# Loads of a softmax in two transfers of 32 KB per partition, on fixed buffers in program order

## The chip, the cores and the metric

The kernel runs on one core of one Trainium2 chip. The metric is the device time of one execution in microseconds (us); smaller is better. An execution under the profiler shows a span about 1.8 us shorter than its device time.

## The reference

Softmax over the last axis of 16 x 256 rows of 32768 float32 values, with a temperature of 1.0:

```python
def reference(logits, temperature):        # logits: 16 x 256 x 32768 float32
    scaled = logits / temperature
    scaled = scaled - scaled.max(axis=-1, keepdims=True)
    exp_scaled = np.exp(scaled)
    return (exp_scaled / exp_scaled.sum(axis=-1, keepdims=True)).astype(np.float32)
```

It reads 537 MB and writes 537 MB, and there is no way round either.

## The kernel before

Each row is cut into two halves, which lie in neighbouring partitions. A tile is 128 partitions x 16384 values, 64 KB in a partition; there are 64 tiles and three buffers for them. A tile is loaded in one transfer, worked on in four pieces of 4096 (maximum on DVE, exponential and sum on ACT), then the factors of its rows are combined, the tile is scaled by DVE and ACT together, and stored in one transfer. Only the first tile's load and the last tile's load and store are cut into four.

```python
def load(i):                       # one transfer, except in the first and last tile
    ...
    for s, n in spans(CW, _LAST_DMA if g in (0, G - 1) else CW):
        tc.keep_in_program_order(nc.sync.dma_start(out=xs[:, s : s + n], in_=x[...]))

def exps(i):
    ...
    for j, (s, n) in enumerate(ps):                    # 4 pieces of 4096
        nc.vector.tensor_reduce(out=nm[:, k : k + 1], in_=xs[:, s : s + n], axis=X, op=A.max, negate=True)
        nc.scalar.activation(out=xs[:, s : s + n], in_=xs[:, s : s + n], func=Exp,
                             bias=nm[:, k : k + 1], scale=inv_t, accum_out=ssum[:, k : k + 1])

def scales(i):
    ...                                                # of each piece 2560 on DVE, 1536 on ACT

# order on the queue: load 0, 1, 2, store 0, then store t, load t + 2 for t = 1, 2, ...
```

All transfers are issued by SP on one queue. Each of the 16 DMA engines does its share of every transfer, in this order.

## Time and profile before

| | before |
|---|---|
| median of the first three runs | 2501.49 us (2500.46 to 2506.35) |
| busy: DVE, ACT | 63%, 55% |
| data rate over the span | 429 GB/s |
| store to store, one tile | 39.1 us |

Two views that the prediction does not show. First, from the page, the costliest group and the issues of the inner tiles; the last number of an issue line is the median time from issue to landing:

```profile
L107 DVE TENSOR_REDUCE nm<-xs 128x1 f32<-128x4096 f32 x256 | 1113.7, 4412 | 661.6 <-DMA xs<-in_logits_dram 661.6
...
out_dram<-xs SPq DMA_DIRECT2D x63, 29.8
xs<-in_logits_dram SPq DMA_DIRECT2D x62, 49.1
```

The maxima are the largest piece of compute, and DVE spends as much as 661.6 us waiting for loads. A store takes some 19 us of transfer but lands 29.8 us after its issue, so about 10 us of other work lay in the queue ahead of it. Call that its **lead**.

### The profile page before, as it was taken

Reading aid. Unit: us, or ns where it says so; the run is one execution under the profiler, and the core shown is the slowest. Engines: PE = TensorE matmul, PEld = TensorE weight load, DVE = VectorE, ACT = ScalarE, POOL = GpSimd, SP = SyncE. Lnnn points to the kernel's source line nnn. Section 1 sums busy time; section 2 is a strip of 40 time slices with the busy share of each in tenths; the row PEclk is TensorE's granted clock in tenths of the full one; section 3 lists DMA queues with packets and bytes.
Section 4 is the critical chain, followed back from the end, with each engine's and each line's share of the span. In section 5 each row is a group of like instructions: output and inputs, shape, how many; then the busy total and the mean of one; then the engine's idle time right before and its main releaser. Section 6 shows DMA issues by size and latency. Waiting matters only on the chain.

```text
span 2504.7 us, 2498 instructions
## 1 busy us (share of the span) xinstructions
DVE 1579.7 (63%) x1216; ACT 1368.7 (55%) x833; POOL 0.2 (0%) x4
## 2 busy tenths in 40 slices
DVE  6575665765656656666565665666657666576665
ACT  5464554645546455464554645546555464564655
POOL 0000000000000000000000000000000000000000
DMA  9999999999999999999999999999999999999998
GB/s 419 434 426 433 429 436 434 436 434 433 435 434 434 429 428 433 433 434 422 433 422 431 434 423 432 433 422 434 429 425 434 423 433 432 423 433 432 423 422 375
DMA packets 19748, 1073.91 MB, mean 429 GB/s; under 512 B 2192, under 2 KB 2192, under 8 KB 2192
## 3 DMA queue, kind: packets, MB, share of 16 engines
q1 hardware_dynamic: 19728, 1073.75, 99.8%
q14 instruction: 20, 0.16, 0.0%
HBM read 536.87 MB, written 536.87 MB: 429 GB/s over the span
## 4 chain that ended last, share of the span: by engine, by line
DMA 74%; DVE 14%; ACT 10%; SPq 1%; issue 0%; ACTq 0%; another core or an unknown queue 0%
DMA xs<-in_logits_dram 72%; DVE nm L107 13%; ACT xs L163 7%; ACT xs L114 3%; DMA out_dram<-xs 2%; SPq L75 1%; DVE xs L160 0%; DVE f L150 0%; ACT ee L131 0%; DVE rS L149 0%; DVE Sh L87 0%; DVE Sh L84 0%; DVE ttj L138 0%; ACTq L224 0%
## 5 line engine op out<-in xcount | busy, mean ns | idle before, releaser
L107 DVE TENSOR_REDUCE nm<-xs 128x1 f32<-128x4096 f32 x256 | 1113.7, 4412 | 661.6 <-DMA xs<-in_logits_dram 661.6
L114 ACT ACTIVATE xs<-xs,nm 128x4096 f32<-128x4096 f32 x256 | 949.1, 3708 | 1032.9 <-DVE nm L107 1032.9
L163 ACT ACTIVATE xs<-xs,f 128x1536 f32<-128x1536 f32 x256 | 382.3, 1564 | 73.5 <-DVE f L150 73.5
L160 DVE TENSOR_SCALAR xs<-xs,f 128x2560 f32<-128x2560 f32 x256 | 380.2, 1549 | 2.6 <-DVE f L150 0.4
L138 DVE CUSTOM_DVE_ANT_0 ttj<-ee,ssum 128x4 f32<-128x4 f32 x64 | 10.4, 162 | 222.4 <-ACT ee L131 222.4
L114 ACT ACTIVATION_READ_ACCUMULATOR xs<-xs,nm 128x1 f32 x256 | 47.8, 187 | 0.0
L131 ACT ACTIVATE ee<-nm,nMh 128x4 f32<-128x4 f32 x64 | 18.0, 282 | 0.0
L150 DVE TENSOR_SCALAR f<-ee,rS 128x4 f32<-128x4 f32 x64 | 14.7, 229 | 2.2
L149 DVE RECIPROCAL rS<-Sh 128x1 f32<-128x1 f32 x64 | 10.5, 164 | 2.2
L87 DVE TENSOR_TENSOR Sh<-Sh 128x1 f32<-128x1 f32 x64 | 10.2, 160 | 2.2
L87 DVE TENSOR_TENSOR nMh<-nMh 128x1 f32<-128x1 f32 x64 | 10.2, 160 | 2.2
L129 DVE TENSOR_REDUCE nMh<-nm 128x1 f32<-128x4 f32 x64 | 10.1, 157 | 2.2
L84 DVE STREAM_SHUFFLE nMh<-nMh 128x1 f32<-128x1 f32 x64 | 9.7, 151 | 0.0
L84 DVE STREAM_SHUFFLE Sh<-Sh 128x1 f32<-128x1 f32 x64 | 9.7, 151 | 0.0
L114 ACT ACT_TABLE_LOAD x1 | 1.3, 1283 | 7.9 <-DMA xs<-in_logits_dram 7.9
L138 DVE DVE_READ_ACCUMULATOR2_ANT Sh<- 128x1 f32 x64 | 5.2, 82 | 0.0
L84 DVE LOAD_MASK_SELECT nMh<-nMh x64 | 0.9, 14 | 2.8
L84 DVE LOAD_MASK_SELECT Sh<-Sh x64 | 0.9, 14 | 2.7
L210 POOL MEMSET const-bfloat16-1.0<- 128x1 bf16 x1 | 0.1, 101 | 0.0
L210 POOL MEMSET const-uint8-127<- 128x1 uint8 x1 | 0.1, 101 | 0.0
L210 POOL MEMSET const-float32-0.0<- 128x1 f32 x1 | 0.1, 98 | 0.2 <-issue 0.2
L210 POOL MEMSET const-float32-1.0<- 128x1 f32 x1 | 0.1, 98 | 0.0
## 6 DMA issues: line engine op xcount, KB each, us to landing
xs<-in_logits_dram SPq DMA_DIRECT2D x8, 2048.0 KB, 27.3
out_dram<-xs SPq DMA_DIRECT2D x4, 2048.0 KB, 15.5
out_dram<-xs SPq DMA_DIRECT2D x63, 29.8
xs<-in_logits_dram SPq DMA_DIRECT2D x62, 49.1
```

The source lines that it names most:

```text
L75: nc.sync.dma_start(out=o[g * P : (g + 1) * P, c * CW + s : c * CW + s + n], in_=xs[:, s : s + n],)
L84: nc.vector.stream_shuffle(out=v[:, j + 1 : j + 2], in_=v[:, j : j + 1], mask=mask)
L87: nc.vector.tensor_tensor(out=v[:, j + 1 : j + 2], in0=v[:, j : j + 1], in1=v[:, j + 1 : j + 2], op=op,)
L107: nc.vector.tensor_reduce(out=nm[:, k : k + 1], in_=xs[:, s : s + n], axis=X, op=A.max, negate=True)
L114: nc.scalar.activation(out=xs[:, s : s + n], in_=xs[:, s : s + n], func=Exp, bias=nm[:, k : k + 1], scale=inv_t, accum_out=ssum[:, k : k + 1],
L129: nc.vector.tensor_reduce(out=nMh[:, 0:1], in_=nm, axis=X, op=A.min)
L131: nc.scalar.activation(out=ee, in_=nm, func=Exp, bias=nMh[:, n_rounds : n_rounds + 1], scale=-1.0,)
L138: nc.vector.tensor_tensor_reduce(out=ttj, in0=ee, in1=ssum, scale=1.0, scalar=0.0, op0=A.mult, op1=A.add, accum_out=Sh[:, 0:1],)
L149: nc.vector.reciprocal(out=rS, in_=Sh[:, n_rounds : n_rounds + 1])
L150: nc.vector.tensor_scalar_mul(out=f, in0=ee, scalar1=rS)
L160: nc.vector.tensor_scalar_mul(out=xs[:, s : s + cut], in0=xs[:, s : s + cut], scalar1=f[:, k : k + 1])
L163: nc.scalar.activation(out=xs[:, s + cut : s + n], in_=xs[:, s + cut : s + n], func=Copy, scale=f[:, k : k + 1],)
```

## The change

The intent: a tile's first half is worked on while its second half is still being loaded, and the schedule is written out in program order on fixed buffers instead of being left to the tile scheduler. The diff, cut to its core:

```diff
-_CW = 16384
 _BUFS = 3
-_PIECE = 4096
-_LAST_DMA = 4096
-_DVE_SHARE = 0.625
+_LOAD = 8192
+_STORE = 16384
+_PIECES = (4096, 4096, 4096, 2048, 2048)
+_ON_DVE = (4096, 4096, 2048, 0, 0)
...
+    buf = [pool.tile([P, W], fp32, tag=f"x{b}", name=f"x{b}") for b in range(_BUFS)]
...
+    def load(t: int) -> None:
+        n = _END if t in (0, G - 1) else _LOAD
+        for s in range(0, W, n):
+            nc.sync.dma_start(out=buf[t % _BUFS][:, s : s + n], in_=x[t * P : (t + 1) * P, s : s + n])
...
+    with tc.manual_schedule():
+        for t in range(_BUFS):
+            load(t)
+        for t in range(G):
+            normalise(t)
+            store(t)
+            if t and t + _BUFS - 1 < G:
+                load(t + _BUFS - 1)
```

The arithmetic is unchanged. The first two pieces lie in the first half of a tile, the other three in the second.

More of the change, by code (lines that the diff above doesn't have):

```diff
@@ L9 @@
 _SPLIT = 2
-_CW = 16384
 _BUFS = 3
-_PIECE = 4096
-_LAST_DMA = 4096
-_DVE_SHARE = 0.625
+_LOAD = 8192
+_STORE = 16384
+_PIECES = (4096, 4096, 4096, 2048, 2048)
+_ON_DVE = (4096, 4096, 2048, 0, 0)
+_END = 4096
+_END_ON_DVE = 2560
+_SETS = 3
 @with_exitstack
@@ L37 @@
     W = V // _SPLIT
-    CW = min(_CW, W)
-    C = W // CW
-    assert W * _SPLIT == V and CW * C == W and (N * _SPLIT) % P == 0
+    assert sum(_PIECES) == W and len(_PIECES) == len(_ON_DVE)
     x = xf.rearrange("n (h v) -> (n h) v", h=_SPLIT)
@@ L43, with store @@
     G = N * _SPLIT // P
-    n_chunks = G * C
+    assert G * P == N * _SPLIT
     n_rounds = _SPLIT.bit_length() - 1
-    xpool = ctx.enter_context(tc.tile_pool(name="x", bufs=_BUFS))
-    spool = ctx.enter_context(tc.tile_pool(name="stats", bufs=3))
-    slots = {}
-    stats = {}
-    def spans(total: int, step: int) -> list[tuple[int, int]]:
-        return [(s, min(step, total - s)) for s in range(0, total, step)]
-    def piece(g: int) -> int:
-        return _PIECE if g < G - 1 else min(_PIECE, _LAST_DMA)
-    def load(i: int) -> None:
-        g, c = divmod(i, C)
-        xs = xpool.tile([P, CW], fp32, tag="x", name="xs")
-        slots[i] = xs
-        for s, n in spans(CW, _LAST_DMA if g in (0, G - 1) else CW):
-            tc.keep_in_program_order(
-                nc.sync.dma_start(
-                    out=xs[:, s : s + n],
-                    in_=x[g * P : (g + 1) * P, c * CW + s : c * CW + s + n],
-                )
-            )
-    def store(i: int) -> None:
-        g, c = divmod(i, C)
-        xs = slots.pop(i)
-        for s, n in spans(CW, _LAST_DMA if g == G - 1 else CW):
-            tc.keep_in_program_order(
-                nc.sync.dma_start(
-                    out=o[g * P : (g + 1) * P, c * CW + s : c * CW + s + n],
-                    in_=xs[:, s : s + n],
-                )
+    K = max(len(_PIECES), W // _END)
+    pool = ctx.enter_context(tc.tile_pool(name="fixed", bufs=1))
+    buf = [pool.tile([P, W], fp32, tag=f"x{b}", name=f"x{b}") for b in range(_BUFS)]
+    widths = dict(nm=K, ssum=K, ee=K, f=K, ttj=K, nMh=2, Sh=2, rS=1)
+    stat = [
+        {
+            k: pool.tile([P, w], fp32, tag=f"{k}{s}", name=f"{k}{s}")
+            for k, w in widths.items()
+        }
+        for s in range(_SETS)
+    ]
+    def load(t: int) -> None:
+        n = _END if t in (0, G - 1) else _LOAD
+        for s in range(0, W, n):
+            nc.sync.dma_start(
+                out=buf[t % _BUFS][:, s : s + n],
+                in_=x[t * P : (t + 1) * P, s : s + n],
+            )
+    def store(t: int) -> None:
+        n = _END if t == G - 1 else _STORE
+        for s in range(0, W, n):
+            nc.sync.dma_start(
+                out=o[t * P : (t + 1) * P, s : s + n],
+                in_=buf[t % _BUFS][:, s : s + n],
             )
@@ L92, in combine, with normalise @@
             )
-    def exps(i: int) -> None:
-        g, c = divmod(i, C)
-        xs = slots[i]
-        ps = spans(CW, piece(g))
-        K = C * len(ps)
-        if c == 0:
-            stats[g] = tuple(
-                spool.tile([P, K], fp32, tag=f"{nm}{K}", name=nm)
-                for nm in ("nm", "ssum", "ee", "f", "ttj")
-            )
-        nm, ssum = stats[g][:2]
-        for j, (s, n) in enumerate(ps):
-            k = c * len(ps) + j
+    def normalise(t: int) -> None:
+        xs = buf[t % _BUFS]
+        if t in (0, G - 1):
+            sizes = [_END] * (W // _END)
+            on_dve = [_END_ON_DVE] * len(sizes)
+        else:
+            sizes, on_dve = _PIECES, _ON_DVE
+        K = len(sizes)
+        at = [sum(sizes[:k]) for k in range(K)]
+        st = stat[t % _SETS]
+        nm, ssum, ee, f, ttj = (st[k][:, :K] for k in ("nm", "ssum", "ee", "f", "ttj"))
+        nMh, Sh, rS = st["nMh"], st["Sh"], st["rS"]
+        for k in range(K):
+            xc = xs[:, at[k] : at[k] + sizes[k]]
             nc.vector.tensor_reduce(
-                out=nm[:, k : k + 1], in_=xs[:, s : s + n], axis=X, op=A.max, negate=True
+                out=nm[:, k : k + 1], in_=xc, axis=X, op=A.max, negate=True
             )
@@ L114, in exps @@
             nc.scalar.activation(
-                out=xs[:, s : s + n],
-                in_=xs[:, s : s + n],
+                out=xc,
+                in_=xc,
                 func=Exp,
@@ L121, in exps @@
             )
-    def factors(g: int) -> None:
-        nm, ssum, ee, f, ttj = stats[g]
-        nMh = spool.tile([P, 1 + n_rounds], fp32, tag="nMh", name="nMh")
-        Sh = spool.tile([P, 1 + n_rounds], fp32, tag="Sh", name="Sh")
-        rS = spool.tile([P, 1], fp32, tag="rS", name="rS")
-        with tc.high_priority():
-            nc.vector.tensor_reduce(out=nMh[:, 0:1], in_=nm, axis=X, op=A.min)
-            combine(nMh, A.min)
-            nc.scalar.activation(
-                out=ee,
-                in_=nm,
-                func=Exp,
-                bias=nMh[:, n_rounds : n_rounds + 1],
-                scale=-1.0,
-            )
-            nc.vector.tensor_tensor_reduce(
-                out=ttj,
-                in0=ee,
-                in1=ssum,
-                scale=1.0,
-                scalar=0.0,
-                op0=A.mult,
-                op1=A.add,
-                accum_out=Sh[:, 0:1],
-            )
-            combine(Sh, A.add)
-            nc.vector.reciprocal(out=rS, in_=Sh[:, n_rounds : n_rounds + 1])
-            nc.vector.tensor_scalar_mul(out=f, in0=ee, scalar1=rS)
@@ L152, in scales @@
-    def scales(i: int) -> None:
-        g, c = divmod(i, C)
-        xs = slots[i]
-        f = stats[g][3]
-        ps = spans(CW, piece(g))
-        for j, (s, n) in enumerate(ps):
-            k = c * len(ps) + j
-            cut = int(n * _DVE_SHARE) // 512 * 512
-            nc.vector.tensor_scalar_mul(
-                out=xs[:, s : s + cut], in0=xs[:, s : s + cut], scalar1=f[:, k : k + 1]
-            )
-            nc.scalar.activation(
-                out=xs[:, s + cut : s + n],
-                in_=xs[:, s + cut : s + n],
-                func=Copy,
-                scale=f[:, k : k + 1],
-            )
@@ L170 @@
-    order = [("L", i) for i in range(min(_BUFS, n_chunks))] + [("S", 0)]
-    for i in range(1, n_chunks):
-        order.append(("S", i))
-        if i + _BUFS - 1 < n_chunks:
-            order.append(("L", i + _BUFS - 1))
-    nxt = 0
-    done = -1
-    loaded = 0
-    for kind, i in order:
-        if kind == "L":
-            load(i)
-            loaded = i + 1
-        else:
-            g = i // C
-            if g > done:
-                while nxt < (g + 1) * C:
-                    assert nxt < loaded
-                    exps(nxt)
-                    nxt += 1
-                factors(g)
-                done = g
-            scales(i)
-            store(i)
+        nc.vector.tensor_reduce(out=nMh[:, 0:1], in_=nm, axis=X, op=A.min)
@@ new lines, in normalise @@
+        combine(nMh, A.min)
+        nc.scalar.activation(
+            out=ee, in_=nm, func=Exp, bias=nMh[:, n_rounds : n_rounds + 1], scale=-1.0
+        )
+        nc.vector.tensor_tensor_reduce(
+            out=ttj,
+            in0=ee,
+            in1=ssum,
+            scale=1.0,
+            scalar=0.0,
+            op0=A.mult,
+            op1=A.add,
+            accum_out=Sh[:, 0:1],
+        )
+        combine(Sh, A.add)
+        nc.vector.reciprocal(out=rS, in_=Sh[:, n_rounds : n_rounds + 1])
@@ new lines, in normalise @@
+        nc.vector.tensor_scalar_mul(out=f, in0=ee, scalar1=rS)
+        for k in range(K):
+            a, b, c = at[k], at[k] + on_dve[k], at[k] + sizes[k]
+            if b > a:
+                nc.vector.tensor_scalar_mul(
+                    out=xs[:, a:b], in0=xs[:, a:b], scalar1=f[:, k : k + 1]
+                )
+            if c > b:
+                nc.scalar.activation(
+                    out=xs[:, b:c], in_=xs[:, b:c], func=Copy, scale=f[:, k : k + 1]
+                )
+    with tc.manual_schedule():
[6 more added lines that the diff above has]
+                load(t + _BUFS - 1)
```

## The prediction

> **What bounds the kernel now.** I read the page from the top: busy shares, then the DMA row, then the chain that ended last, and after that the waits and one stretch of the timeline. The busy shares say that no engine is the bound (DVE 63%, ACT 55%); the DMA rows say what is.
>
> ```profile
> DVE 1579.7 (63%) x1216; ACT 1368.7 (55%) x833; POOL 0.2 (0%) x4
> ...
> DMA  9999999999999999999999999999999999999998
> ...
> q1 hardware_dynamic: 19728, 1073.75, 99.8%
> ...
> HBM read 536.87 MB, written 536.87 MB: 429 GB/s over the span
> ...
> DMA 74%; DVE 14%; ACT 10%; SPq 1%; issue 0%; ACTq 0%; another core or an unknown queue 0%
> ```
>
> One queue keeps the 16 DMA engines occupied for 99.8% of the span, with no slice below 9 tenths but the last. The chain names DVE and ACT for 24%, but a chain follows one path only; while it runs through DVE the DMA engines are busy too. Whether compute really holds up the transfers has to be seen in one steady tile. The timeline there:
>
> ```profile
> 1008.18 0.33 SPq L75 DMA_DIRECT2D out_dram<-xs  x1
> 1008.56 0.43 SPq L64 DMA_DIRECT2D xs<-in_logits_dram  x1
> 1018.79 17.40 DVE L107 TENSOR_REDUCE nm<-xs 128x1 f32<-128x4096 f32 x4 [10.72 <-DMA xs<-in_logits_dram]
> ...
> 1041.30 5.94 DVE L160 TENSOR_SCALAR xs<-xs,f 128x2560 f32<-128x2560 f32 x4
> 1041.36 5.97 ACT L163 ACTIVATE xs<-xs,f 128x1536 f32<-128x1536 f32 x4 [1.15 <-DVE f L150]
> 1047.36 0.33 SPq L75 DMA_DIRECT2D out_dram<-xs  x1
> 1047.74 0.43 SPq L64 DMA_DIRECT2D xs<-in_logits_dram  x1
> 1057.69 17.40 DVE L107 TENSOR_REDUCE nm<-xs 128x1 f32<-128x4096 f32 x4 [10.45 <-DMA xs<-in_logits_dram]
> ```
>
> Call a row block of 128 x 16384 values (8.39 MB) a tile. A tile lands at 1018.79, is computed in 28.57 us, and its store is issued at 1047.36. The load issued at 1008.56 lands only at 1057.69. So when the store is put into the queue, the queue still has 1057.69 - 1047.36 = 10.3 us of loading ahead of it: compute is early by that much. The wait views agree:
>
> ```profile
> DVE nm L107 <- DMA xs<-in_logits_dram: 661.6, 65, 22.3
> ...
> SPq L75 <- DVE xs L160: 2385.2, 67, 38.7
> ...
> SPq L64 <- DMA out_dram<-xs: 13.0, 2, 10.8
> ```
>
> DVE waits for loads 65 times, some 10 us a tile. SP waits nearly always for the scaling, which is harmless because the queue behind it is full; it waits for a buffer to be stored only twice, at the start. The kernel is bound by the rate of its transfers, from the first packet to the last.
>
> **The steady period.** Stores go out at 1008.18 and 2415.83, 36 tiles apart: 39.10 us a tile. How long does a transfer take undisturbed? At the start the waits of DVE end at 7.89, 12.78, 17.67 and 22.57, so a 2.1 MB transfer (16 KB a partition) takes 4.90 us; the next, 8.39 MB (64 KB), lands at 41.91: 19.34 us. A load and a store would then be 2 x 19.34 = 38.68. The missing 0.42 us a tile (27 us in 64 tiles) is the change of direction: in the trace's packet records a 64 KB packet takes 2.418 us nearly always, and the longer ones (up to some 3.7 us) are mostly the last of a load with a store behind it. The semaphore records show too that the 16 DMA engines drift apart: from 0.3 us between first and last at the start to about 8.5 us from the middle on. The last of them sets the time, and it never runs dry.
>
> **What the Trainium skill says.** Three places. "DMA: Bandwidth & Descriptors", Where 436 GB/s comes from: a fabric ceiling of 435.2 GB/s. This trace agrees: 8.39 MB in 19.34 us is 433.7 GB/s. At the ceiling 1073.74 MB would need 2467 us (an estimate from the page's figure), 1.4% under the time now, so a gain over 2% isn't there to be had with the same bytes. Same page, Why small descriptors are slow: a fixed overhead for each packet of about 3 cycles. The trace agrees that there is one: packets of 16 KB take 611 ns and of 64 KB 2418 ns; on a straight line that is about 9 ns fixed. "Perfetto Trace Analysis", DMA Optimizations: splitting may let work start sooner "if DMA engines are generally idle". Here they are not, so the condition fails.
>
> **The change part by part.**
> 1. *Loads in two transfers of 32 KB a partition.* 62 tiles change (the first and the last keep four of 16 KB). On the line through 4.90 us for 2.1 MB and 19.34 us for 8.39 MB, 4.19 MB takes 4.90 + (19.34 - 4.90)/3 = 9.71 us, two of them 19.42: 0.08 us more than one. The packet records give the same: 16 x (611 + (2418 - 611)/3 = 1213 ns) + 2 x 9 for the semaphores, against 8 x 2418 + 9, is +73 ns. All of it lies on the bound: 62 x 0.08 = **+5 us**.
> 2. *Compute starts on the first half.* Two reductions of 4.41 us (8.8 us) then run in the 9.7 us before the second half lands. After it lands: reductions of 4096, 2048, 2048, the last three exponentials, factors, scaling. By the rows now, an ACT pass takes 3.71 us for 4096 and (on the line with 1.56 for 1536) about 2.0 for 2048. So: first reduction done at 4.4, exponentials with their reads until 4.4 + 3.9 + 2.2 + 2.2 = 12.7, factors until about 14.1, scaling 6.0 (ACT 3 x 1.99; DVE 2 x 2.35 + 1.28): about **20 us** instead of 28.6. Stores are issued 8.5 us earlier in the period, with about 19 us in the queue ahead of them instead of 10.3. As the queue never was empty, this is worth **0 us**; DVE and ACT only idle longer.
> 3. *More instructions:* 5 pieces for 4, fewer scale operations. DVE a tile: 3 x 4.41 + 2 x 2.28 + 5.98 + about 1.5 = 25.3 us against 24.7; ACT 22.3 against 21.4. Both stay far below 39.1: **0 us**.
> 4. *Fixed buffers, program order.* Still three buffers of 64 KB, and the SP order store t, load t+2 is the old one. A load needs the store of the tile two before the last stored one landed, some 20 us after the last landing. That is now about when the next store goes out (20 us), so SP will wait for stores in nearly every tile, briefly. At that moment the queue still holds most of a load and a whole store: **0 us**.
> 5. *Start and end.* The first four loads and the last four stores keep their sizes; the last engine had no gap there before: **0 us**.
>
> Sum: 2501.5 + 5 = 2506.5; I put 2507.
>
> **The rivals.**
> *The change of direction gets cheaper or dearer.* It is 27 us now. The last packet before a store is half as long; if the extra time goes with packet size, 13 us come back and the time is about 2493. Against it: what is lost looks like a cost of turning round, and there are as many turns as before. The other way: with the store waiting in the queue for longer (19 us), or the engines drifting further apart (by my model the leaders can be 39.1 - 20 - 2 = 17 us ahead, now 39.1 - 28.6 - 2 = 8.5, which matches what is seen), the last engine could lose more. The first turn in the trace, with its store queued 23 us early, cost some 1 us. Half as much again each turn would be +13: about 2520.
> *A wait takes the place of the one removed.* SP stuck on a load's buffer holds back the store behind it. For this to cost anything the queue must run dry for the last engine, and it has over 15 us in it. If it did happen at 1 us a tile: 2570.
> *DVE or ACT becomes the bound.* At 25.3 and 22.3 us of 39.1 this can't be, unless program order makes them wait in turn; 20 us after a landing leaves 19 to spare.
> *The transfers were held up by compute after all,* so that the extra slack buys back the 27 us: about 2479. The leaders do wait for stores to be issued, but the last engine doesn't, and only it counts. I give it little.
>
> **Range and chances.** The known term is +5; the unknown one is the turn, within about -13 and +13; repeated runs before spread by 6 us. So 2495 to 2520 for 8 in 10. Faster by over 2% (below 2451) is under the ceiling's 2467: 0.5%. Slower by over 2% (above 2552) needs a stall I can't find: 2.5%. The rest is within 2%.
>
> **What would show it.** Right: DMA still 9 tenths throughout; packets 19728 + 62 x 144 = 28656 on the queue; halves landing 9.7 us apart; a period of about 39.2 us; store issued about 20 us after the second half; SP waits for stores in some 60 places, short. DVE's wait for loads split in two per tile. Wrong: a period under 38.9 (turns cheaper) or over 39.5 (turns dearer, drift), DMA slices below 9 tenths (starved), or SP waiting longer for stores than the queue is deep.

## More of the kernel before

Every run here was at a granted clock of 1.0. The experiments ran in three sets, each on its own chip (1 to 4, 5 to 8, 9 to 11), and runs of the kernel before were mixed into each: 2495.97 to 2509.48 us over all of them. Differences of a few us are safe within a set, less so between sets.

Second, the busy times in two stretches of the steady part; the columns are the stretch, its length, busy us of DVE, ACT and POOL with their counts, granted clock, DMA share and GB/s:

```profile
400.00:1500.00 1100.00, 698.39 (x534) 605.05 (x367) 0.00 (x0) 1.00 1.00 432
1500.00:2400.00 900.00, 568.29 (x438) 491.88 (x301) 0.00 (x0) 1.00 1.00 430
```

The DMA share is 1.00 in both, and still the rate differs a little. A share of 1.00 says that packets were under way, not that they moved as fast as they can.

## The result, and the profile after

The changed kernel took 2496.48 us in the median of four runs (2496.34 to 2496.77), the kernel before 2502.43 us (2500.46 to 2506.35). The ratio is 0.9974, with a 95% interval of 0.9957 to 0.9992: a quarter of a per cent faster, and much steadier. (The fastest of all runs of the kernel before, 2495.97 us, is as fast; it is its other runs that are slower. A ratio here is the mean time of one kernel's fast runs over that of the other's in the same rounds, so it is not quite the ratio of the medians quoted.) The profiled spans were 2504.7 and 2494.7 us. The profiled run of the kernel before, 2506.49 us, was slower than its four timed ones, so the 10 us between the profiles are more than the usual gain of some 6.

The queues and the chain after, from the page:

```profile
q1 hardware_dynamic: 28656, 1073.75, 99.7%
q14 instruction: 22, 0.18, 0.0%
HBM read 536.87 MB, written 536.87 MB: 430 GB/s over the span
...
DMA 73%; ACT 13%; DVE 12%; another core or an unknown queue 1%; SPq 1%; issue 0%; ACTq 0%
```

There are 28656 packets instead of 19728, just the 62 x 144 more that were expected, and DMA is as full as before. The steady tile in the timeline after:

```profile
1017.04 8.80 DVE L103 TENSOR_REDUCE nm<-x 128x1 f32<-128x4096 f32 x3 [0.93 <-DMA x<-in_logits_dram]
...
1030.55 5.81 DVE L139 TENSOR_SCALAR x<-x,f 128x4096 f32<-128x4096 f32 x3
1030.61 5.79 ACT L143 ACTIVATE x<-x,f 128x2048 f32<-128x2048 f32 x3 [1.15 <-DVE f L135]
1036.43 0.34 SPq L71 DMA_DIRECT2D out_dram<-x  x1
1036.82 0.91 SPq L63 DMA_DIRECT2D x<-in_logits_dram  x2
1046.06 8.74 DVE L103 TENSOR_REDUCE nm<-x 128x1 f32<-128x4096 f32 x2 [9.70 <-DMA x<-in_logits_dram]
...
1055.74 8.80 DVE L103 TENSOR_REDUCE nm<-x 128x1 f32<-128x4096 f32 x3 [0.94 <-DMA x<-in_logits_dram]
...
1075.13 0.34 SPq L71 DMA_DIRECT2D out_dram<-x  x1
```

The second half of a tile lands at 1017.04 and its store is issued 19.4 us later, at 1036.43. The next tile's second half lands at 1055.74, so this store has a lead of 19.3 us instead of 10.3. From store to store it is 38.70 us. Who waited, DVE first and then the queue of SP:

```profile
DVE nm L103 <- DMA x<-in_logits_dram: 673.3, 128, 17.6
```

```profile
SPq L71 <- DVE x L139: 1780.2, 67, 33.5
SPq L71 <- DMA x<-in_logits_dram: 571.0, 60, 18.0
SPq L63 <- DMA out_dram<-x: 28.0, 11, 15.3
```

DVE waits for loads as long as before in all, only twice a tile. SP waits for a store to land 11 times, 28 us in all. And the two stretches of the steady part again:

```profile
400.00:1500.00 1100.00, 700.81 (x548) 608.83 (x401) 0.00 (x0) 1.00 1.00 433
1500.00:2400.00 900.00, 570.95 (x439) 493.81 (x324) 0.00 (x0) 1.00 1.00 433
```

The second stretch moves 433 GB/s, where it was 430: there, at a DMA share that never left 1.00, is the gain.

**Where it lies.** Each transfer ends with one semaphore increment from each of the 16 DMA engines, and the trace records them. The time between the last increments of two transfers is what the last engine needed. Its undisturbed time for a tile is 38.63 us with one load and 38.70 with two (the shortest tiles of these profiles and those below). What it lost on top:

- Before: some 28 us in all. Ten steps of about 0.95 us, some 250 us apart, and the rest, about 18 us, in losses of 0.1 to 0.7 us (1.0 in the first) in most of the other loads, mostly in the packet or two ahead of the store.
- After: some 13 us. About 4 us in the first eight tiles, then hardly anything but nine steps of 1.0 us.

So 14 us of losses at the turn from load to store went and the added packets took 4 us back: 10 us, as the spans say. The timeline agrees: over the last 59 stores a tile took 39.07 us before and 38.89 after, 10.6 us in all. But why are the losses gone? The same turn from load to store still happens in every tile.

The increments show one more thing. The 16 engines start together and drift apart; the time between the first and the last is called the **distance** below. Before, the first was ahead of the last by 0.3 us at the start, and from the middle on by 8 to 9.6 us, no further. After, the distance grows by 1.0 us at each step and reaches 12.3 us. So before, something held the first ones back.

### The profile page after: what moved, and what is told of

It is laid out like the page before. It is cut to its first block, busy times and chain, and to the rows that moved or that the text cites. A ratio compares the mean times of both kernels' runs of the same rounds, so it can differ in the third digit from the quotient of the medians.

```text
span 2494.7 us, 2743 instructions
## 1 busy us (share of the span) xinstructions
DVE 1581.4 (63%) x1216; ACT 1367.8 (55%) x895; POOL 0.2 (0%) x4
## 3 DMA queue, kind: packets, MB, share of 16 engines
q1 hardware_dynamic: 28656, 1073.75, 99.7%
## 4 chain that ended last, share of the span: by engine, by line
DMA 73%; ACT 13%; DVE 12%; another core or an unknown queue 1%; SPq 1%; issue 0%; ACTq 0%
DMA x<-in_logits_dram 64%; DVE nm L103 11%; DMA out_dram<-x 8%; ACT x L110 7%; ACT x L143 6%; SPq L71 0%; DVE f L135 0%; ACT ee L120 0%; DVE rS L134 0%; DVE Sh L82 0%; DVE ttj L123 0%; DVE Sh L79 0%; SPq L63 0%; ACTq L185 0%
## 5 line engine op out<-in xcount | busy, mean ns | idle before, releaser
L103 DVE TENSOR_REDUCE nm<-x 128x1 f32<-128x4096 f32 x318 | 1123.3, 3581 | 673.3 <-DMA x<-in_logits_dram 673.3
L110 ACT ACTIVATE x<-x,nm 128x4096 f32<-128x4096 f32 x318 | 965.4, 3036 | 1020.9 <-DVE nm L103 1020.9
L143 ACT ACTIVATE x<-x,f 128x2048 f32<-128x2048 f32 (+1 forms) x194 | 370.9, 1975 | 73.7 <-DVE f L135 73.7
L139 DVE TENSOR_SCALAR x<-x,f 128x4096 f32<-128x4096 f32 (+2 forms) x194 | 372.2, 1975 | 2.3
L123 DVE CUSTOM_DVE_ANT_0 ttj<-ee,ssum 128x5 f32<-128x5 f32 (+1 forms) x64 | 10.6, 166 | 196.7 <-ACT ee L120 196.7
L110 ACT ACTIVATION_READ_ACCUMULATOR x<-x,nm 128x1 f32 x318 | 59.3, 186 | 0.0
L120 ACT ACTIVATE ee<-nm,nMh 128x5 f32<-128x5 f32 (+1 forms) x64 | 18.1, 284 | 0.0
L135 DVE TENSOR_SCALAR f<-ee,rS 128x5 f32<-128x5 f32 (+1 forms) x64 | 14.8, 231 | 2.2
L118 DVE TENSOR_REDUCE nMh<-nm 128x1 f32<-128x5 f32 (+1 forms) x64 | 10.1, 158 | 2.2
```

Source lines behind the costliest of these rows:

```text
L103: nc.vector.tensor_reduce(out=nm[:, k : k + 1], in_=xc, axis=X, op=A.max, negate=True)
L110: nc.scalar.activation(out=xc, in_=xc, func=Exp, bias=nm[:, k : k + 1], scale=inv_t, accum_out=ssum[:, k : k + 1],)
L118: nc.vector.tensor_reduce(out=nMh[:, 0:1], in_=nm, axis=X, op=A.min)
L120: nc.scalar.activation(out=ee, in_=nm, func=Exp, bias=nMh[:, n_rounds : n_rounds + 1], scale=-1.0)
L123: nc.vector.tensor_tensor_reduce(out=ttj, in0=ee, in1=ssum, scale=1.0, scalar=0.0, op0=A.mult, op1=A.add, accum_out=Sh[:, 0:1],)
L135: nc.vector.tensor_scalar_mul(out=f, in0=ee, scalar1=rS)
```

## The experiments

Theories at the start: SIZE (a turn costs in proportion to the last load packet, and that was halved), LEAD (it costs because the store is queued late) and ORDER (fixed buffers and program order did it).

**1. Undo the split of the loads alone** (load64).

```diff
-_LOAD = 8192
+_LOAD = 16384
```

> Only the split of the loads is undone (one transfer of 64 KB per partition); fixed buffers, program order and the five pieces stay. The load-to-store turn cost the last DMA engine about 16 us before and about 3 us after. Theory SIZE (the turn costs in proportion to the last load packet, 64 KB against 32 KB) and theory LEAD (it costs because the store is queued only 10 us ahead of the turn, against 19 us): both expect the turn's cost back and the 5 us of packets gone, 2501 to 2504 us, with losses of 0.1 to 0.6 us in most loads. Theory ORDER (fixed buffers and program order removed it): stays near 2491 us.

Measured: 2497.66 us, but spread over 2494.83 to 2509.60; ratio 0.9986 (0.9967 to 1.0005), so not to be told from the kernel before, whose 11 runs in this set lay between 2498.63 and 2507.51. The profile holds the hint. Between about 600 and 1500 us its tiles take 38.63 us each but for the steps of 1 us, without any loss at a turn; from about 1550 us on losses of 0.1 to 0.7 us come back, when the first engine is 9 us ahead of the last. A large packet alone costs nothing at a turn, so SIZE is in trouble.

**2. Keep the split, start the compute late** (late_start). The pieces of the second half are taken first:

```diff
-        for k in range(K):
+        late = [k for k in range(K) if at[k] >= W // 2] + [k for k in range(K) if at[k] < W // 2]
+        for k in late:
             xc = xs[:, at[k] : at[k] + sizes[k]]
```

> Loads stay in two halves, but the pieces of the second half are worked on first, so that compute starts only when the whole tile is there and the store is queued some 10 us ahead of the turn, as before. SIZE: still 2496 us, no loss at turns after the first tiles. LEAD: the turn's cost is back on top of the packets, 2504 to 2509 us.

Measured: 2503.60 us (2503.17 to 2505.21), ratio 1.0005. With the small packets and the whole rest of the change in place, the gain is gone. SIZE and ORDER fall. (Some 2 us of the time are lost at the very end, where the last store has to wait for the last tile's compute; the rest is losses at turns.) The profile says more. Its two stretches:

```profile
400.00:1500.00 1100.00, 701.28 (x536) 608.96 (x399) 0.00 (x0) 1.00 1.00 433
1500.00:2400.00 900.00, 567.35 (x442) 492.01 (x325) 0.00 (x0) 1.00 1.00 429
```

and stores issued in each of them, from the timeline of the SP queue:

```profile
734.48 0.34 SPq L71 DMA_DIRECT2D out_dram<-x  x1
...
773.19 0.34 SPq L71 DMA_DIRECT2D out_dram<-x  x1
...
811.89 0.34 SPq L71 DMA_DIRECT2D out_dram<-x  x1
...
2175.74 0.34 SPq L71 DMA_DIRECT2D out_dram<-x  x1
...
2214.97 0.34 SPq L71 DMA_DIRECT2D out_dram<-x  x1
...
2253.76 0.34 SPq L71 DMA_DIRECT2D out_dram<-x  x1
```

Tiles of 38.71 and 38.70 us early on, of 39.23 and 38.79 later, in one run and with the same lead of some 10 us throughout. So it isn't the lead of the last engine by itself either. What had changed was the distance between first and last: it grew by a step at a time and stopped at about 8.3 us near 1480 us, and there the losses began. A store with 10.3 us of lead on the last engine has only 2 us on an engine that is 8.3 us ahead: that one comes to the store almost as soon as it is issued, and if it came any sooner it would have to wait. Call this theory **STARVE**: once the engines ahead have caught up with the issue of the stores, the last one loses at its turns. (The expectations below say "run dry", which is stronger; the packet records, after experiment 11, show how far that is so.)

**3. One load, but a shorter path to the store** (load64_short; a wrong result):

```diff
-                    out=xs[:, a:b], in0=xs[:, a:b], scalar1=f[:, k : k + 1]
+                    out=xs[:, a:a+64], in0=xs[:, a:a+64], scalar1=f[:, k : k + 1]
```

and the same on ACT, with one load as in 1.

> Wrong result on purpose: one load of 64 KB per partition, and the scaling writes only 64 columns of each stretch, so that the store is queued about 6 us earlier than in the run with one load (lead some 16 us, not 10) with the same instructions. SIZE: as the run with one load, 2501 to 2504 us. LEAD: the turn's cost goes without the packets of the split, 2489 to 2493 us.

Measured: 2492.97 us (2491.90 to 2496.49), ratio 0.9964. Lead in the profile: 15.6 us. The distance grows to 12.9 us and isn't stopped, and after the first 26 transfers there are next to no losses but the steps. More lead is worth having without any split. The ranges of 1 and 3 overlap a little, and the short scaling also spares DVE and ACT some work; experiment 2 changes the lead without that.

**4. The split alone, in the kernel before** (before_split):

```diff
-        for s, n in spans(CW, _LAST_DMA if g in (0, G - 1) else CW):
+        for s, n in spans(CW, _LAST_DMA if g in (0, G - 1) else CW // 2):
```

in the load only.

> The kernel before with one part of the change alone: loads of the inner tiles in two transfers of 32 KB per partition, four pieces and the scheduler's order as before. SIZE and LEAD: 2495 to 2498 us, as the changed kernel. ORDER: 2505 to 2508 us (the packets' 5 us on top of the kernel before).

Measured: 2496.07 us (2495.74 to 2496.49), ratio 0.9974, as the whole change. The other parts (fixed buffers, program order, five pieces) add nothing that shows here.

**5. One load, and a longer path to the store** (load64_long):

```diff
         nc.vector.tensor_scalar_mul(out=f, in0=ee, scalar1=rS)
+        nc.vector.tensor_reduce(out=ttj[:, 0:1], in_=xs[:, 0:4096], axis=X, op=A.max)
```

> One load of 64 KB, and one spare reduction of 4096 (4.4 us) ahead of the scaling, so that the store is queued some 6 us ahead of the last engine's turn instead of 10.6. Theory STARVE (the last engine loses at its turn only once the engines ahead of it have run dry and wait for the store to be issued): the spread between first and last engine stops at about 4 us instead of 9, the losses begin before the tenth tile and go on in most tiles, 2501 to 2508 us. Theory CHANCE (the losses are unrelated to the lead, load64 was merely lucky): 2495 to 2500 us, spread up to 9 us.

Measured: 2518.55 us (2517.04 to 2520.06), ratio 1.0061. A steady tile in its timeline:

```profile
1957.92 0.33 SPq L71 DMA_DIRECT2D out_dram<-x  x1
...
1997.00 0.33 SPq L71 DMA_DIRECT2D out_dram<-x  x1
...
2003.51 17.46 DVE L103 TENSOR_REDUCE nm<-x 128x1 f32<-128x4096 f32 x5 [6.58 <-DMA x<-in_logits_dram]
```

The lead is 6.5 us, the tile 39.08 us. The distance between the engines stopped at 5 to 6 us, and nearly every load had a loss, from the start on, most of 0.3 to 0.6 us. The direction and the pattern are as STARVE has them; the size was underrated, by 10 us and more. About 3 us of that is at the end, where the last stores now wait for the last tile's compute. The queue of the last engine still held 6.5 us of work whenever a store was issued, and DVE waited for loads for 6.6 us of the tile shown: 4.4 us of compute that should have been hidden made the kernel 21 us slower than experiment 1 (some 19 by the ratios, since the two ran in different sets).

**6. The split, and more lead still** (split_short; a wrong result): the change, with the scaling cut short as in 3.

> Wrong result on purpose: the changed kernel, with the scaling writing only 64 columns of each stretch, so that stores are queued some 5 us earlier still (lead 25 us, not 19). STARVE: nothing more to gain, no engine ran dry before either; 2495.5 to 2497 us. Theory LEAD in proportion (each us of lead is worth about 0.8 us): 2492 us.

Measured: 2495.87 us (2495.34 to 2496.63), ratio 0.9972, at a lead of 24.3 us. No gain over a lead of 19.3. Lead is worth something until no engine catches up, and then nothing: STARVE, not lead in proportion.

**7. Loads in four** (load16):

```diff
-_LOAD = 8192
+_LOAD = 4096
```

> Loads of all tiles in four transfers of 16 KB per partition. The packet term alone: 32 packets of 611 ns and 4 semaphore packets against 16 of 1213 and 2, 0.16 us a tile, 10 us in 62 tiles: 2505 to 2508 us, no losses at turns after the first tiles. If packets cost nothing: 2496 us.

Measured: 2502.75 us (2502.44 to 2503.63), ratio 1.0000. Slower by 6.3 us than the change, not by 9 to 11. The undisturbed transfers did come to 10.7 us more in the trace; but the losses were some 4 us smaller, with fewer and smaller steps. Why these shrink was not followed up.

**8. Split only the later tiles** (split_late_tiles):

```diff
-        n = _END if t in (0, G - 1) else _LOAD
+        n = _END if t in (0, G - 1) else (W if t < 32 else _LOAD)
```

(in the load).

> Tiles 1 to 31 loaded in one transfer, tiles 32 to 62 in two. In the run with one load the engines ahead did not run dry before about tile 40, so by STARVE the split isn't needed earlier: no losses after the first tiles, and 31 x 0.08 = 2.5 us of packets saved: 2493 to 2495 us. If the engines run dry before tile 32: 2496 to 2500 us.

Measured: 2495.54 us (2493.64 to 2498.64), ratio 0.9971. A little above what was expected, and no longer steady: there are a few losses at turns before tile 32, and no clear gain over the change.

**9 and 10. What are the steps of 1 us?** The packet records have packets of 8192 bytes on the instruction queue, among others at 1074.6, 1346.4 and 1579.6 us of the changed kernel. In just these places the last engine lost 1.0 us (stores landing at 1076.0, 1347.9 and 1581.1). Each of its nine steps has such a packet; after the first tiles, the other packets of that queue go with no loss of the last engine. The guess: the last engine is the one that also fetches the instructions of one engine, probably of DVE, since a tile has 19 of those and a step comes every 6 to 7 tiles. Fewer (few) and twice as many (many) DVE instructions:

```diff
-_PIECES = (4096, 4096, 4096, 2048, 2048)
-_ON_DVE = (4096, 4096, 2048, 0, 0)
+_PIECES = (8192, 4096, 4096)
+_ON_DVE = (8192, 2048, 0)
```

```diff
             normalise(t)
+            spare(t)      # 19 times: nc.vector.tensor_scalar_mul on one column
             store(t)
```

> The changed kernel with three pieces (8192, 4096, 4096) and two DVE scale operations, 16 DVE instructions a tile instead of 19. Store still queued some 17 us ahead, so no engine runs dry. Theory FETCH (what is left of the last engine's losses is 1.0 us each time a packet of DVE instructions is fetched through its ring): the steps of 1.0 us come every 7.7 tiles instead of every 6.5, one or two fewer: 2494.5 to 2496 us. Otherwise unchanged at 2496.5 us.

> The changed kernel with 19 spare DVE operations of one column (some 3 us) after the scaling of each tile, which double the DVE's instructions. FETCH: steps of 1.0 us every 3.3 tiles, about nine more, 2503 to 2507 us, with DVE far from being the bound and DMA still full. If instructions are fetched for nothing: 2496.5 us.

Measured: few 2495.40 us (2494.68 to 2495.59), ratio 0.9965; many 2505.86 us (2505.26 to 2506.33), ratio 1.0007. The instruction queue (packets, MB, share) on the page of few, then on that of many, there with the group of the spare operations:

```profile
q14 instruction: 18, 0.15, 0.0%
```

```profile
q14 instruction: 32, 0.26, 0.0%
...
L150 DVE TENSOR_SCALAR ttj<-rS 128x1 f32<-128x1 f32 x1216 | 186.1, 153 | 39.7
```

The changed kernel had 22 such packets; fewer and more instructions make 18 and 32.

The count is of all engines' instructions; the steps tell more of DVE's. Few has eight steps of 1.0 us, every 7 to 8 tiles; many has one every three to four, and 9 us more time, though its spare operations come after the scaling and keep no store back. With many the distance between the engines reached 17 to 18 us, at a lead of about 19, and there, over the last sixth of the run, small losses at turns came back: STARVE once more, at another distance. Few is the fastest correct version that was steady here; its range does not touch the changed kernel's, but they ran in different rounds and the gain is 0.04%.

**11. Stores in two as well** (store32):

```diff
-_STORE = 16384
+_STORE = 8192
```

> The changed kernel with the stores of the inner tiles also in two transfers of 32 KB per partition. The packet term on the store side: 63 x 0.08 us = 5 us, no other change: 2500 to 2503 us. If the losses at the turn go with the size of the store's packet: below 2497 us.

Measured: 2498.47 us (2497.64 to 2499.49), ratio 0.9978: 2.0 us slower than the change, less than the 4 to 6 expected. Its steps were mostly of 0.65 to 0.8 us; the losses at turns did not go further down with the store's packet. They even went up: fifteen loads between 395 and 1100 us lost 0.1 to 0.5 us each, 3.7 us in all, at a lead of about 21 us and a distance of only 4 to 10. No engine was near to catching up there, so STARVE does not explain these.

**What the packet records add.** They carry no engine's number, but the 16 chains can be put together: the packets of an engine follow each other within nanoseconds, in an order of sizes that the program fixes (36 to 56 of the 20000 to 28000 records found no clear place in the first four rows below, up to 355 in the last). Whether the engines ahead have caught up can then be read from the time between a store's issue and the start of its first packet on any engine. For tiles 8 to 61, with the mean loss of the last engine at the turn from load to store, steps of 1 us left out:

| run | tiles with a first packet under 2 us after the issue | loss there, us | loss in the other tiles, us |
|---|---|---|---|
| before | 40 of 54, from 891 us on | 0.33 | 0.17 |
| late start (2) | 27 of 54, from 1395 us on | 0.24 | 0.03 |
| one of 64 KB, longer path (5) | 54 of 54 | 0.43 | |
| many (10) | 11 of 54, from 2014 us on | 0.11 | 0.02 |
| the change, split alone, both short ones | none | | 0.01 to 0.02 |

The losses go with the catching up. "Run dry" in the full sense is rarer: three or more engines without a packet around the issue were found in only 6, 3, 7 and 2 of the 54 tiles of the first four rows, and in none of the last. (In the kernel before, all six come right after a step of 1 us, which puts the last engine, the compute and the next issue back, but not the engines ahead.) In the other tiles the engines ahead mostly go from load to store without a gap. But they have bunched, mostly 10 to 15 of them within 0.5 us where it was 4 to 8 before they caught up, and they lose time too, in the last packet of the store, ahead of the next load: in the kernel before none of these packets was over 0.08 us too long in the first 22 tiles, and from tile 24 on 11 of the 16 were in the median tile.

The main runs side by side, in order of the lead (the first and the last row are from another set than the middle ones, and the change from the first runs):

| loads | lead, us | distance between engines | median, us |
|---|---|---|---|
| one of 64 KB, longer path | 6.5 | stopped at 5 to 6 | 2518.55 |
| two of 32 KB, late start | 10.3 | stopped at about 8.3 | 2503.60 |
| one of 64 KB | 10.6 | stopped at about 9 | 2497.66 (up to 2509.60) |
| one of 64 KB, short | 15.6 | 12.9, growing to the end | 2492.97 |
| two of 32 KB (the change) | 19.3 | 12.3, growing to the end | 2496.48 |
| two of 32 KB, short | 24.3 | 12.1, growing to the end | 2495.87 |

**What stays open.** That the last engine loses once the others have caught up is shown by when the losses begin, in four profiles, at distances of 5, 8, 9 and 17 us that follow the lead, and by the experiments that shorten or lengthen the lead. How this makes the last one slower, in its last load packets, is not shown: the waiting, the bunching, or the engines ahead turning to stores at once could each do it. Nor is it shown why the kernel before lost 0.1 to 0.4 us in many loads already between 450 and 900 us, when its distance was still 4 to 8 us, or store32 in its first half; the run with one load lost nothing between 600 and 1500 us. So catching up is one way to lose at a turn, not the only one. And the turns of the first tiles cost up to 1 us each in all kernels, while the engines are still close together.

## Why the prediction was right or wrong

The time, 2496.5 us, lies in the range of 2495 to 2520, near its lower end, and "within 2%" was the class given 97%. The sign of the small difference was not what the sum said: +5 us were predicted, about -6 measured (-10 between the profiled runs). That the range held, by 1.5 us, was partly luck: it had been opened downwards for a rival (smaller packets at the turn) that the experiments refute. A sign of being wrong that the prediction named did come, though barely: "a period under 38.9 (turns cheaper)"; it was 38.89 on average over the last 59 stores and 38.70 in the tile shown.

- *The bound.* Right: the transfers, before and after. The line through two durations predicted the halves well: 9.7 us apart in the trace, and 38.70 us for an undisturbed tile.
- *Part 1, the packets.* Right: 0.08 us a tile predicted, 0.07 measured (38.70 against 38.63), 4.3 us in 62 tiles. With about the same lead, two loads against one cost 5.9 us (experiments 2 and 1), but 2 of these are the end of late start, and the runs with one load spread over 15 us.
- *Part 2, the earlier compute.* Its times were right (store after "about 20 us", measured 19.4; lead 19, measured 19.3). Its worth was the step that failed: "As the queue never was empty, this is worth 0 us". The queue was never empty for the last engine; but the engines ahead had caught up with the issue of the stores in 40 of 54 tiles, from 891 us on, and were now and then without work. The same error stands in the last rival: "The leaders do wait for stores to be issued, but the last engine doesn't, and only it counts". It does count, but it pays when the others have caught up. In this term belongs some -5.5 us in place of 0: experiment 4 against 2, which ran together, is -7.5, and 2 of these are the end of late start. With the packets' +4 the sum would have come near -1 (-6 measured in the medians, with a spread of 6 us in the kernel before), and with the 14 us of the two profiles to their -10.
- *Part 3, busy times.* 25.3 and 22.3 us a tile were predicted for DVE and ACT; the page gives 1581.4 / 64 = 24.7 and 1367.8 / 64 = 21.4. A little high, and of no consequence.
- *Part 4, waits of SP.* Waits for stores were expected in nearly every tile; there were 11. Store and need were expected at the same moment, 20 us after a landing, and mostly the store was down just before. No cost, as predicted.
- *The rival of the turn.* It named the 27 us (28 by the count above) but the wrong reasons. The long packets were read as "mostly the last of a load with a store behind it": so it is on the last engine, but of all 64 KB packets that took over 0.08 us too long in that trace, 402 were the last of a store and 236 the last of a load, and the former belong to the engines ahead. That was the trace of catching up. Packet size does not matter (experiment 2), and a longer lead makes turns cheaper, not dearer. Ten of the 27 us weren't the turn at all but the fetching of instructions.
- *The model of the distance,* lead less about 2 us, held in the four kernels where the distance stopped. (The changed one never came to its 17 us; it ended at 12.3, since the distance grows by 1 us in 6 to 7 tiles.) It was in the prediction, and the use it could have been put to was missed.

## What to carry to other kernels

Where the DMA engines are the bound, find out how far ahead of its turn a transfer is put into the queue, and compare that with how far the 16 engines have drifted apart; "the queue is never empty" has to hold for the first engine, with some 2 us to spare here, and not only for the last. Buying that lead with smaller transfers costs a little (0.07 us a tile here), and more lead than the drift needs buys nothing. Instructions are data too: here nine packets of 8 KB of instructions, DVE's by experiments 9 and 10, each took a microsecond from the engine that set the time.

## What the Trainium skill lacked or had wrong

- "DMA: Bandwidth & Descriptors", Why a DMA increments its semaphore by 16 and not by 1, says that a transfer runs on up to 16 engines that finish independently. Its section Latency and other measured facts notes that two of them are usually slower in traces, with a guess at the cause that belongs to transfers issued from GpSimd; here SP issued them all. What is lacking is how far the engines drift apart over a long kernel (0.3 us at the start, 5 to 18 us later in these runs), and that the last one loses once the first have caught up with the issue of the stores: 433 GB/s before that, 429 after, in one run (experiment 2).
- The same page, Queues, rings and completion order, lists row 14 as runtime-internal, refill among it, without a cost; "Runtime: NRT & Kernel Launch", Instruction fetch mechanics, calls the cost of fetching the next block of instructions "mostly hidden". Here it was not hidden from a kernel that is bound by its transfers: a packet of 8 KB on the instruction queue took 1.0 us from the last engine, about nine times in a run, and doubling DVE's instructions cost 9 us (experiment 10).
- "Perfetto Trace Analysis", DMA Optimizations, ties splitting to DMA engines that are "generally idle". Here they were 99.8% busy and the split still gained 6 us in the median, not by filling idle time but because the stores were queued before the engines ahead came to them.
